# A weight stream's buffers moved to 224 bytes beyond a multiple of 256

## The chip, the cores and the metric

The kernel runs on one core of one Trainium2 chip. The metric is device time in microseconds from the first to the last instruction of one execution with what lies around them, the median over several executions. Smaller is better. Before the change it is 773.04 us (three runs, 772.54 to 774.1).

## The reference, cut to what matters

One hybrid encoder layer over 512 tokens and 16 meta tokens, width 1024, all in float32:

```python
h = rmsnorm(x, mix_norm)
na_q, na_k, na_v, df_q, df_k, df_v, g_na, g_df = split(h @ w_in)      # 40 blocks of 128 columns
o_na = neighbourhood_attention(na_q, na_k, na_v, na_rpb) @ w_na_out   # 8 heads of 64
o_df = diff_attention(rope(df_q), rope(df_k), df_v, lam) @ w_diff_out # 4 heads, two softmaxes each
x = x + (sigmoid(g_na) * o_na + sigmoid(g_df) * o_df) @ w_o
h = rmsnorm(x, ffn_norm)
x = x + (silu(h @ w_gate) * (h @ w_up)) @ w_down                      # D_FF = 2816
return rmsnorm(x, final_norm)[:, 16:]
```

## The kernel before

Every activation is kept transposed, with 128 channels on the partitions and the tokens along the row. Every large product is written as three matmuls in a rounded float32 type: operands are split into a rounded half (`whi`, `xh`, `mh` and so on) and a remainder (`wlo`, `xl`, `ml`), and `mm3` issues high by high (L140), high by low (L142) and low by high (L144) into one accumulator. In a matmul the weight block is loaded into the array (a LDWEIGHTS on PEld), and the activation is streamed through it (the MATMUL on PE): in `pg<-xh,wlo` the output is `pg`, the stream `xh`, the loaded weights `wlo`.

The work has these stages:

- Attention. Eight units (four heads of differential attention, four pairs of neighbourhood attention) in turn; beside each runs the dense projection of the next: k and v (`pk`, `pv`, tokens in two runs of 256 and 272 columns), q (`pq`, 512) and a gate block (`pg`, 512). A generator hands out dense steps between attention slots.
- `diff_out` (`pd`), the other branch's projection (`pn`) and the output projection (`po`), all with 512 columns.
- SwiGLU: for each of 22 blocks of 128 columns, seven half-size products (256 columns) from the operands `xb` (Strassen's scheme over gate and up weights).
- Down projection (`pdn`, 512 columns; the last block in two halves, `pdh`, 256 columns), then the final norm.

The pool `wp` is the weight stream. A piece of 128 x 1024 floats (512 KB) is loaded by SyncE into one of three buffers of the tag `wraw` (as `wraw`, as `fG` for the gate weights of the SwiGLU, as `draw` for the down weights). ACT then writes its rounded half and DVE the remainder:

```python
raw = self.wp.tile([P, 8, P], F32, name="wraw", tag="wraw", bufs=3)
hi = self.wp.tile([P, 8, P], F32R, name="whi", tag="whi", bufs=2)
lo = self.wp.tile([P, 8, P], F32R, name="wlo", tag="wlo", bufs=2)
nc.scalar.copy(hi[:, k:k + h], raw[:, k:k + h])
eng.tensor_tensor(out=lo[:, k:k + h], in0=raw[:, k:k + h], in1=hi[:, k:k + h].bitcast(F32), op=ALU.subtract)
```

In attention and the projections all loaded weights are `whi` and `wlo`. In the SwiGLU two of the seven products (`PB11` into `pa`, `PB21` into `pb`) use them; the other five use tiles of a pool `F` (`fwh`, `fsh`, `fdh` and their remainders). In the down projection the first two pieces lie in them (as `dhi`, `dlo`), the others in a ring (`wring`).

Where tiles lie. Pools are stacked from the low end of each partition: constants, small tiles, `wp` at byte 10,496 = 41 x 256, then the pools after it. Other pools are stacked from the high end, under a pad of 56 floats that brings them to multiples of 256. All buffers of `wp` are of 4096 bytes, so each begins on a multiple of 256. So do the streamed operands: rows of `xh` and `xl` are padded to 576 floats (2304 bytes), `mh`, `ml`, `onh`, `odh`, `gh` and `gl` are of whole multiples. The exception is `xb`, which starts 8 floats into its tile; the ring takes the same space from its start:

```python
xbt = [XB.tile([P, nxb + 64], F32R, name="xb", tag=t) for t in ("xbh", "xbl")]
xbh, xbl = (t[:, 8:8 + nxb].rearrange("p (i k n) -> p i k n", i=7, k=4) for t in xbt)
```

Of the kernel before, what the change touches and what calls it, by code (L numbers as in the profile page):

```python
# [10 lines left out]
F32 = mybir.dt.float32  # L11
# [7 lines left out]
P = 128  # L19
# [52 lines left out]
class Kernel:  # L72
# [665 lines left out]
    def run(self):  # L738
        tc, nc, a = self.tc, self.nc, self.a
        es = ExitStack()  # L740
        self.cp = es.enter_context(tc.tile_pool(name="cp", bufs=1))
        self.sm = es.enter_context(tc.tile_pool(name="sm", bufs=1))
        self.wp = es.enter_context(tc.tile_pool(name="wp", bufs=1))
        sA2 = ExitStack()
        A2 = sA2.enter_context(tc.tile_pool(name="A2", bufs=1))
        self.od = A2.tile([P, 4, T], F32, name="od")
        self.onh = A2.tile([P, 4, T], F32R, name="onh")
        self.onl = A2.tile([P, 4, T], F32R, name="onl")
        self.gates = A2.tile([P, 8, T], F32, name="gates")
        sA1 = ExitStack()  # L750
        self.A1 = sA1.enter_context(tc.tile_pool(name="A1", bufs=1))
        sat = ExitStack()
        self.attn = sat.enter_context(tc.tile_pool(name="attn", bufs=1))

        rp = es.enter_context(tc.tile_pool(name="rp", bufs=1, side="right"))
        nc.gpsimd.memset(rp.tile([P, 56], F32, name="pad"), 0.0)
        self.sstg = ExitStack()
        self.stg = self.sstg.enter_context(tc.tile_pool(name="stg", bufs=1, side="right"))
        self.sM2 = ExitStack()
        sps = ExitStack()  # L760
        self.pjp = sps.enter_context(tc.tile_pool(name="pjp", bufs=3, space=PSUM))
        self.tp = sps.enter_context(tc.tile_pool(name="tp", bufs=2, space=PSUM))
        self.mp = sps.enter_context(tc.tile_pool(name="mp", bufs=1, space=PSUM))
        self.sp = sps.enter_context(tc.tile_pool(name="sp", bufs=1, space=PSUM))

        self.setup()
        self.sts = [dict() for _ in range(8)]
        self.late = False
        self.cur = -1

        self.bms = []
        for _ in self.dense_first():
            pass
        self.stream = self.stream_a()
        for i in range(8):
            st = self.sts[i]
            self.drain_until(lambda: "ready" in st)
            self.cur = i
            for s in range(8):
                for fn in self.pend.pop(self.slot, []):  # L780
                    fn()
                self.fill(FILL_A)
                if i % 2 == 0:
                    self.d_scores(i // 2, st, s)
                    if s in (1, 4):
                        self.bms.append(self.build_bm(i + (s == 4)))
                else:
                    self.n_scores(i // 2, st, s)
                self.fill(FILL_B)
                self.slot += 1  # L790
        while self.pend:
            for fn in self.pend.pop(self.slot, []):
                fn()
            self.fill(FILL_A + FILL_B)
            self.slot += 1
        self.late = True
        for _ in self.stream:
            pass
        sat.close()
        sps.close()  # L800
        sA1.close()
        self.phase_b(sA2)
        self.sM2.close()
        es.close()
# [414 lines left out]
```

## Time and profile before

| | |
|---|---|
| median of 3 runs | 773.04 us (772.54 to 774.1) |
| profiled execution, its time | 773.11 us |
| its span, first to last instruction | 771.3 us |
| mean granted TensorE clock | 0.986 |
| attention with its projections | up to 320 us |
| `pd`, `pn`, `po` | 320 to 408 us |
| SwiGLU | 408 to 632 us |
| down projection and final norm | 634 to 771 us |

The span is what the trace covers; the 1.8 us that the execution takes beyond it lie around the first and last instruction. In the rows of the profile that follow, times are in microseconds from the start of the span, and means of one instruction are in nanoseconds. A matmul's duration is a latency: the next one starts before it ends, so how fast a row of matmuls goes is read from their starts.

### The profile page before, as it was taken

To read this page: it belongs to the slowest core of one execution; us is meant where nothing else is said; L and a number is where in the kernel's file an instruction comes from. 1 tells how busy PE (TensorE), PEld (TensorE's weight loads), DVE (VectorE), ACT (ScalarE), POOL (GpSimd) and SP (SyncE) were. 2 spreads that over 40 slices of the span, in tenths; PEclk is the share of its full clock that TensorE was granted. 3 is DMA by queue.
4 is the path that set the end of the run, shared out by engine and by line. 5 is a ranking of instruction groups with operands and counts; after the bars stand their busy time and mean duration, and the time that the engine had idled before them with its cause. 6 is when DMAs were issued, how large, how long until landed. Compare 5 with 4: busy or idle time off the path is not lost.

```text
span 771.3 us, 12598 instructions
## 1 busy us (share of the span) xinstructions
PE 748.6 (97%) x4794; PEld 674.1 (87%) x4794; DVE 575.6 (75%) x1053; ACT 379.7 (49%) x669; POOL 55.3 (7%) x141
## 2 busy tenths in 40 slices
PE   7999999999999999999998999999999989999995
PEld 5899889998889888878887999999999987888884
DVE  5777897788788867648889899999999959632214
ACT  6345545545554546514554655555555556422201
POOL 2030110110011000001121000000000000000100
PEclk8999999999999999999998999999999999999998
DMA  7474643453563412235541333333333232633003
GB/s 261 136 182 143 158 123 103 123 152 104 137 159 101 121 58 80 82 110 163 169 132 42 110 110 110 110 107 104 104 104 108 66 102 68 206 103 95 1 1 109
DMA packets 34715, 87.88 MB, mean 114 GB/s; under 512 B 4512, under 2 KB 6576, under 8 KB 34656
## 3 DMA queue, kind: packets, MB, share of 16 engines
q1 hardware_dynamic: 32688, 82.97, 35.6%
q0 software_dynamic: 1136, 3.34, 1.5%
q8 instruction: 37, 0.61, 0.3%
q10 hardware_dynamic: 832, 0.79, 0.3%
q14 instruction: 22, 0.18, 0.1%
HBM read 70.01 MB, written 2.10 MB: 93 GB/s over the span
## 4 chain that ended last, share of the span: by engine, by line
PE 85%; DVE 9%; DMA 2%; issue 1%; ACT 1%; SPq 0%; DVEq 0%; ACTq 0%
PE pdn L144 4%; PE pdn L140 4%; PE pdn L142 4%; PE pa L140 4%; PE pa L144 4%; PE pb L140 4%; PE pg L140 4%; PE pa L142 4%; PE pb L142 4%; PE pb L144 4%; PE pg L144 4%; PE pg L142 4%; PE s L513 2%; PE pv L140 2%; PE pv L142 2%; PE pv L144 2%
## 5 line engine op out<-in xcount | busy, mean ns | idle before, releaser
L117 ACT CAST whi<-wraw 128x1024 fp32r<-128x1024 f32 (+1 forms) x57 | 58.9, 1033 | 56.9 <-PE pd L142 13.1
L118 DVE TENSOR_TENSOR wlo<-wraw,whi 128x1024 fp32r<-128x1024 f32 (+1 forms) x57 | 68.5, 1201 | 17.2 <-ACT whi L117 16.9
L144 PE MATMUL pdn<-gh,wring 128*128 128x512 f32 x138 | 53.8, 390 | 1.3 <-DVE wring L155 1.3
L140 PE MATMUL pdn<-gh,wring 128*128 128x512 f32 x138 | 53.8, 390 | 0.0
L142 PE MATMUL pdn<-gl,wring 128*128 128x512 f32 x138 | 53.7, 389 | 0.0
L140 PE MATMUL pg<-xh,whi 128*128 128x512 f32 x128 | 52.6, 411 | 0.4 <-DVE vt L379 0.4
L142 PE MATMUL pg<-xl,whi 128*128 128x512 f32 x128 | 50.6, 395 | 0.0
L144 PE MATMUL pg<-xh,wlo 128*128 128x512 f32 x128 | 50.2, 393 | 0.0
L155 DVE TENSOR_TENSOR wring<-draw,wring 128x1024 fp32r<-128x1024 f32 (+1 forms) x22 | 24.7, 1126 | 28.8 <-ACT wring L154 28.8
L154 ACT CAST wring<-draw 128x1024 fp32r<-128x1024 f32 (+1 forms) x22 | 21.0, 974 | 45.9 <-PE pdn L142 34.5
L154 ACT CAST fdh<-fG 128x1024 fp32r<-128x1024 f32 x22 | 23.2, 1056 | 36.8 <-PE pa L142 34.7
L154 ACT CAST ath<-tp 128x256 fp32r<-128x256 f32 (+1 forms) x48 | 20.5, 443 | 42.2 <-PE tp L637 22.0
L1137 POOL TENSOR_TENSOR ssq<-ssq,sq 128x512 f32<-128x512 f32 x11 | 16.4, 1493 | 345.6 <-ACT sq L1136 335.2
L155 DVE TENSOR_TENSOR wlo<-fG,whi 128x1024 fp32r<-128x1024 f32 x22 | 26.9, 1224 | 14.4 <-ACT whi L154 14.4
L517 ACT ACTIVATE e<-s,m 128x528 f32<-128x528 f32 x32 | 22.5, 704 | 23.0 <-DVE m L515 22.7
L144 PEld LDWEIGHTS pdn<-gh,wring 128*128 128x128 f32 x138 | 25.9, 188 | 7.1 <-DVE wring L155 1.7
L140 PE MATMUL pk<-xh,whi 128*128 128x256 f32 (+1 forms) x128 | 28.9, 303 | 3.1 <-ACT xh L244 3.1
L140 PEld LDWEIGHTS pdn<-gh,wring 128*128 128x128 f32 x138 | 25.9, 188 | 5.6 <-ACT wring L154 0.2
L142 PEld LDWEIGHTS pdn<-gl,wring 128*128 128x128 f32 x138 | 25.9, 188 | 5.3
L155 DVE TENSOR_TENSOR fwl<-fW,fwh 128x1024 fp32r<-128x1024 f32 x22 | 26.9, 1225 | 3.1 <-ACT fwh L154 3.1
L144 PEld LDWEIGHTS pg<-xh,wlo 128*128 128x128 f32 x128 | 24.0, 188 | 5.2
L621 ACT ACTIVATE en<-en,m 128x272 f32<-128x272 f32 x32 | 16.7, 522 | 24.1 <-DVE m L619 23.8
(292 smaller groups left out, 2596.2 us busy)
## 6 DMA issues: line engine op xcount, KB each, us to landing
wraw<-in_w_in_dram SPq DMA_DIRECT2D x39, 512.0 KB, 3.8
fG<-in_w_gate_dram SPq DMA_DIRECT2D x22, 512.0 KB, 3.5
kd<-khl SPq DMA_DIRECT2D x32, 264.0 KB, 4.2
draw<-in_w_down_dram SPq DMA_DIRECT2D x16, 512.0 KB, 3.6
fW<-in_w_up_dram SPq DMA_DIRECT2D x22, 256.0 KB, 2.6
fV<-in_w_up_dram SPq DMA_DIRECT2D x22, 256.0 KB, 2.9
qs<-qhl SPq DMA_DIRECT2D x32, 128.0 KB, 2.8
wraw<-in_w_o_dram SPq DMA_DIRECT2D x8, 512.0 KB, 3.5
```

The costliest lines, as they stand in the source:

```text
L117: nc.scalar.copy(hi[:, k:k + h], raw[:, k:k + h])
L118: eng.tensor_tensor(out=lo[:, k:k + h], in0=raw[:, k:k + h], in1=hi[:, k:k + h].bitcast(F32), op=ALU.subtract)
L140: nc.tensor.matmul(outs[i], wh, rhs[i][0], start=start, stop=False, **kw)
L142: nc.tensor.matmul(outs[i], wh, rhs[i][1], start=False, stop=False, **kw)
L144: nc.tensor.matmul(outs[i], wl, rhs[i][0], start=False, stop=stop, **kw)
L154: self.nc.scalar.copy(hi, src)
L155: self.nc.vector.tensor_sub(lo, src, hi.bitcast(F32))
L513: nc.tensor.matmul(sc[:, r0:r1], qs[:, q], kd[:, p, r0:r1], start=p == 0, stop=p == 1)
L517: nc.scalar.activation(e, sc, AF.Exp, bias=m, accum_out=l[:, c:c + 1])
L621: x = nc.scalar.activation(e[:, :n], e[:, :n], AF.Exp, bias=m, scale=-1.0, accum_out=l[:, 0:1])
L1137: (nc.gpsimd if m < n - 1 else nc.vector).tensor_tensor(out=ssq, in0=ssq, in1=sq, op=ALU.add)
```

## The change

A pad of 56 floats (224 bytes) becomes the first tile of `wp`, and a pool with a pad of 8 floats (32 bytes) follows `wp`. The stream's seven buffers then begin at 10,720 and every 4096 bytes after it, 224 bytes beyond a multiple of 256; what is stacked behind them begins 256 bytes higher than before, on the same place within 256. Tiles at the high end stay. The pads are written once each by POOL, as the allocator wants a tile that is used.

```diff
         self.cp = es.enter_context(tc.tile_pool(name="cp", bufs=1))
         self.sm = es.enter_context(tc.tile_pool(name="sm", bufs=1))
         self.wp = es.enter_context(tc.tile_pool(name="wp", bufs=1))
+
+        nc.gpsimd.memset(self.wp.tile([P, 56], F32, name="wpad"), 0.0)
+        wpe = es.enter_context(tc.tile_pool(name="wpe", bufs=1))
+        nc.gpsimd.memset(wpe.tile([P, 8], F32, name="wpad2"), 0.0)
         sA2 = ExitStack()
         A2 = sA2.enter_context(tc.tile_pool(name="A2", bufs=1))
```

On PE, DVE, ACT and SyncE the instructions and their order are those of before. POOL's order before, from the kernel's first instructions to the setup of the constants (`vec` holds the norm weights):

```order
L1203 MEMSET const-uint8-127 128x1
L1212 UNCONDITIONAL_BRANCH
L756 MEMSET pad 128x56
L214 DMA vec<-in_vec_dram 128x25
L262 MEMSET ones_d 128x1
```

And now, at the same place:

```order
L1207 MEMSET const-uint8-127 128x1
L1216 UNCONDITIONAL_BRANCH
L745 MEMSET wpad 128x56
L747 MEMSET wpad_69 128x8
L760 MEMSET pad 128x56
L214 DMA vec<-in_vec_dram 128x25
L262 MEMSET ones_d 128x1
```

The two new MEMSETs stand ahead of the load of `vec`; lines behind the change are numbered four higher.

## The prediction

> **What bounds the kernel now.** I read the page first: the busy shares, then the chain of work that ended last.
>
> ```profile
> PE 748.6 (97%) x4794; PEld 674.1 (87%) x4794; DVE 575.6 (75%) x1053; ACT 379.7 (49%) x669; POOL 55.3 (7%) x141
> ...
> PE 85%; DVE 9%; DMA 2%; issue 1%; ACT 1%; SPq 0%; DVEq 0%; ACTq 0%
> ```
>
> TensorE is busy 97% of the span and is 85% of the chain. Busy matmuls overlap, so I next took the table by stage. Its columns are the stretch, its length, then busy time and instruction count of PE, PEld, DVE, ACT and POOL, then the granted clock, the DMA share and GB/s.
>
> ```profile
> 33.00:320.00 287.00, 286.69 (x1797) 254.15 (x1798) 231.43 (x584) 152.18 (x321) 29.45 (x92) 1.00 0.44 123
> 364.70:408.00 43.30, 43.30 (x193) 35.85 (x192) 36.47 (x49) 25.56 (x40) 8.21 (x7) 1.00 0.44 141
> 423.00:630.00 207.00, 207.00 (x1771) 206.52 (x1770) 182.85 (x226) 118.07 (x192) 0.00 (x0) 1.00 0.32 104
> 650.00:742.00 92.00, 92.00 (x408) 76.14 (x407) 33.88 (x38) 26.39 (x31) 6.95 (x5) 1.00 0.33 99
> ```
>
> These are attention with its projections, the output projection, the SwiGLU products and the down projection. PE is full in all four at clock 1.00, so the kernel's time is the number of matmuls times the time from one start to the next. That step is what a moved operand could change, and I read it from start times in the timeline (first and last of a run; the count between them follows each row pair).
>
> ```profile
> 700.21 0.39 PE L140 MATMUL pdn<-gh,wring 128*128 128x512 f32 x1
> ...
> 702.93 0.39 PE L140 MATMUL pdn<-gh,wring 128*128 128x512 f32 x1
> ```
> ```profile
> 307.41 0.39 PE L142 MATMUL pg<-xl,whi 128*128 128x512 f32 x1
> ...
> 308.57 0.39 PE L140 MATMUL pg<-xh,whi 128*128 128x512 f32 x1
> ...
> 310.83 0.39 PE L142 MATMUL pg<-xl,whi 128*128 128x512 f32 x1
> ```
> ```profile
> 747.22 0.28 PE L140 MATMUL pdh<-gh,wring 128*128 128x256 f32 x1
> ...
> 748.06 0.28 PE L142 MATMUL pdh<-gl,wring 128*128 128x256 f32 x1
> ```
> ```profile
> 500.03 0.28 PE L140 MATMUL pa<-xb,fsh 128*128 128x256 f32 x1
> ...
> 501.43 0.28 PE L140 MATMUL pb<-xb,whi 128*128 128x256 f32 x1
> ```
> ```profile
> 120.05 0.41 PE L140 MATMUL pv<-xh,whi 128*128 128x256 f32 x2
> ...
> 122.49 0.28 PE L142 MATMUL pv<-xl,whi 128*128 128x256 f32 x1
> ```
>
> - 512 columns, steady: 12 steps in 2.72 us, 226.7 ns each.
> - 512 columns just after other work: 5 steps in 1.16 us, 232 ns; the next 10 take 2.26 us, 226 ns. After a break the row needs some five matmuls to settle.
> - 256 columns in the last block (`pdh`): 7 steps in 0.84 us, 120.0 ns.
> - 256 columns in the SwiGLU (`xb`): 12 steps in 1.40 us, 116.7 ns.
> - 256 and 272 columns alternating (`pk`, `pv`): 10 pairs in 2.44 us, 244 ns a pair.
>
> From 226.7 and 120.0 a column costs 106.7/256 = 0.417 ns, and a matmul 13.3 ns besides. The same sum leaves 10.0 ns for `xb`, 18.6 ns for the unsettled 512s, and 12.0 ns for each of a pair. The kernel tells `xb` from `pdh` by one thing that bears on this change: `xb` starts 8 floats (32 bytes) into a tile that lies on a multiple of 256, while `gh` and `gl` lie on one. So where the streamed (moving) operand lies seems to be worth 3.3 ns a matmul. The change moves the other operand, the loaded weights.
>
> **The change part by part.** *Which matmuls read a moved tile.* The `whi`/`wlo` (and `dhi`/`dlo`) halves feed them. The rows below are one of three products each (L140, L142, L144), columns as on the page.
>
> ```profile
> L144 PE MATMUL pg<-xh,wlo 128*128 128x512 f32 x128 | 50.2, 393 | 0.0
> L144 PE MATMUL pa<-xb,wlo 128*128 128x256 f32 x88 | 25.1, 285 | 0.0
> L144 PE MATMUL pq<-xh,wlo 128*128 128x512 f32 x64 | 25.1, 392 | 0.0
> L144 PE MATMUL po<-mh,wlo 128*128 128x512 f32 x64 | 24.9, 389 | 0.0
> L144 PE MATMUL pb<-xb,wlo 128*128 128x256 f32 x88 | 24.6, 279 | 0.0
> L144 PE MATMUL pk<-xh,wlo 128*128 128x256 f32 x64 | 18.5, 289 | 0.0
> L144 PE MATMUL pv<-xh,wlo 128*128 128x256 f32 x64 | 18.2, 284 | 0.0
> L144 PE MATMUL pn<-onh,wlo 128*128 128x512 f32 x32 | 12.5, 389 | 0.0
> L144 PE MATMUL pd<-odh,wlo 128*128 128x512 f32 x32 | 12.4, 389 | 0.0
> L144 PE MATMUL pdn<-gh,dlo 128*128 128x512 f32 x16 | 6.2, 390 | 0.0
> ```
>
> With 512 columns: (128+64+64+32+32+16) x 3 = 1008. In pairs: `pk` and `pv`, 64 of 256 columns and as many of 272, x 3: 768. In the SwiGLU: (88+88) x 3 = 528, two of its seven products. That is 2304 of 4794; the rest, the ring weights of the down projection above all, stay where they were.
>
> *The weight load itself.* One row has loads at odd places already: the mean square of x reads 88-column slices of one tile, so that slice c begins 352c bytes in, at 0, 96, 192, 32, 128 and 224 bytes beyond a multiple of 256.
>
> ```profile
> 25.56 0.70 PEld L181 LDWEIGHTS ms<-ones_d,ssq 128*88 128x88 f32 x8 [0.18 <-issue]
> ```
> ```profile
> L181 PEld LDWEIGHTS ms<-ones_d,ssq x20: 153/158/333, 25.6 to 417.9; 128*88 128x88 f32 x12, 128*128 128x128 f32 x8
> ```
>
> Eight loads (two for each slice) in 0.70 us: less the last one's 0.158, 7 steps of 77 ns. The 12 loads have a median of 158 and a minimum of 153 (the row's maximum is of its 128-column form). None stands out, so a load that begins 32 or 224 bytes off costs nothing that shows when it runs alone. Beside 512 columns a load has room: PEld is busy 76.14 of the 92.00 us of the down projection. Beside 256 it has none to spare, at 206.52 of 207.00 us in the SwiGLU. What is not shown is a wide stream and a shifted load together. Bounds, in ns a matmul: as the settled and unsettled 512s differ, +5.3 on 1008, +5.3 us; as `pdh` and `xb` differ in the good direction, -3.3 on 1008 and 12.0 to 10.0 on 768, -3.4 - 1.5 = -4.9 us. I take 0, the row of loads alone being nearest to what is moved: the weights.
>
> *The splits that write the halves.* ACT casts 80 pieces (56 of attention and the projections, 22 of the gate weights, 2 of the down weights) and DVE subtracts as many, now from and to shifted tiles. `xb` is written at 32 bytes off, `mh` and `wring` are not:
>
> ```profile
> L154 ACT CAST mh<-m 128x512 fp32r<-128x512 f32 x8 | 5.0, 621 | 15.0 <-DVE m L838 15.0
> L154 ACT CAST xb<-xg 128x512 fp32r<-128x512 f32 x4 | 2.4, 604 | 0.0
> L155 DVE TENSOR_TENSOR xb<-xt,xb 128x768 fp32r<-128x768 f32 x4 | 3.8, 955 | 1.8 <-ACT xb L154 1.8
> L155 DVE TENSOR_TENSOR wring<-draw,wring 128x768 fp32r<-128x768 f32 x8 | 7.7, 958 | 10.8 <-ACT wring L154 10.8
> ```
>
> 604 against 621 and 955 against 958: nothing on either engine, and both lie beside PE.
>
> *The transfers.* All of `wraw`, `fG` and `draw` now land off a multiple of 256.
>
> ```profile
> wraw<-in_w_in_dram SPq DMA_DIRECT2D x39, 512.0 KB, 3.8
> ```
> ```profile
> SPq L104 <- DVE wlo L118: 142.1, 32, 8.3
> ```
> ```profile
> ACT whi L117 <- DMA wraw<-in_w_in_dram: 4.9, 2, 3.5
> ```
> ```profile
> 2.13 6.98 DMA wraw<-in_w_in_dram
> ```
>
> A piece lands 3.8 us after its issue, but the queue waited 142.1 us for DVE to free a buffer, so the stream runs ahead of its use; ACT waited for it twice, 4.9 us. In the output projection a piece is used each 43.3/8 = 5.4 us with three buffers. Even at twice 3.8 us it would be there in time. The queue is in order, so what stands behind a slower piece (the copies of k and q) would start later by the same, with the same slack. The one landing on the path is the first piece, 6.98 us of the start. Bounds: 0, and, for a tenth more on 6.98, 0.7 us. I take 0: nothing in the rows shows a landing that depends on its place. The Trainium skill, DMA: Bandwidth & Descriptors, "How a descriptor splits into AXI transactions", speaks against the change: a transfer that starts off a 256-byte boundary pays for a whole first transaction. By that, an estimate: 4096 bytes from 224 on make 17 transactions of 135 beats in place of 16 of 128, 5.5% more; on the first landing 0.4 us, so that the sum would be 773.5. The waits above show why it would end there; no row of this profile shows packets by their place.
>
> *Two MEMSETs on POOL,* ahead of the load of `vec`:
>
> ```profile
> 0.74 0.14 POOL L756 MEMSET pad<- 128x56 f32 x1 [0.29 <-POOLq L1203]
> 1.30 0.68 POOL L214 DMA_DIRECT2D vec<-in_vec_dram  x1 [0.41 <-issue]
> ```
> ```profile
> vec<-in_vec_dram POOLq DMA_DIRECT2D x1, 12.5 KB, 3.6
> ```
>
> At most 0.14 us each, less where they overlap as POOL's others do. `vec` is wanted by ACT's first scaling, which stands behind the cast of the piece that lands at 2.13 + 6.98 = 9.1 us; issued at 1.30 and landed 3.6 us later, it has some 4 us to spare. Nothing. *The tiles behind the stream* move by 256 bytes, the same place within 256, and the settled step is the same for operands at many multiples of it: nothing.
>
> **Sum.** 773.11 us for the profiled execution (span 771.3 and 1.8 around it) + 0 = 773.1; the median of the runs, 773.04, is 0.07 below it, which I neglect.
>
> **The rivals.**
> 1. *Slower: the shifted load keeps the 512-column rows from settling.* The five steps of 232 ns show that such a state exists with nothing else different; if the load's place decides it, the state would last. For it: 512-column matmuls are the ones that settle to a better step. Against it: the load has long ended before the next matmul starts. 1008 x 5.3 = +5.3: 778.4. It decides when the step of `po` stays over 228.
> 2. *Slower: the load of the SwiGLU's two products takes longer beside a stream.* PEld has no slack there; 116.7 would become 120.0 as for `pdh`: 528 x 3.3 = +1.7, 774.8.
> 3. *Faster: it is the distance between stream and weights that counts.* `xb` lies 32 bytes ahead of its weights modulo 256; with the weights at 224, `xh`, `mh` and the others lie just so too. Then each matmul's 13.3 (pairs 12.0) would become 10.0: -4.9, 768.2; if only the pairs gain, -1.5, 771.6. Against it: nothing separates the distance from the place of the stream alone, and the loads alone show no effect. The Trainium skill, TensorE: Matmul & The Clock Gate, "Step-by-step: what each phase is for", says that weights and stream have independent read ports and that a load does not steal from the running matmul. By that rule neither 1 nor 3 could come and the time would be the forecast's; no row here shows it either way.
>
> **How the numbers follow.** What a measurement of this kernel can tell from no change is about 0.2%, 1.5 us. Forecast (773.1, with the landing term up to 773.8): 0.45, the most, since the loads alone are the only rows with the moved operand off its place. Rival 1: 0.21; rival 2: 0.11, its 1.7 being just past the bound; rival 3: 0.23, of which a third gains only on the pairs and ends near the bound. So faster 0.22, same 0.46, slower 0.32. The range reaches to both outer cases, 768.2 and 778.4, as each is likelier than one in ten; what is left out is a sum of a rival and a transfer term beyond them: 768.0 to 778.6. The forecast alone: 772.5 to 774.1, its terms and the spread of the runs shown (772.54 to 774.1).
>
> **What the profile after would show.** Steps: 226.7 in `po`, 120.0 in `pdh`, 116.7 in `pb` from `wlo`, 244 a pair in `pv`, all as now; 228 or more in `po` is rival 1, 120 in the `wlo` products of the SwiGLU alone is rival 2, 223 or 240 a pair is rival 3. The casts of ACT and the subtractions of DVE keep their means. A landing time of `wraw` over 3.8 us with more than 4.9 us of ACT's waits would show the transfers at work. I would be wrong if the weights' place within 256 sets the step of a matmul in either direction.

## The result, and the profile after

| | before | after |
|---|---|---|
| median | 773.04 us (7 runs, 772.39 to 774.1) | 776.43 us (7 runs, 775.32 to 778.65) |
| ratio to before | | 1.0048, interval 1.0033 to 1.0063 |
| profiled execution, span | 771.3 us | 774.5 us |

The kernel became slower by 3.4 us. The busy shares and the chain of the changed kernel's page:

```profile
PE 753.2 (97%) x4794; PEld 674.3 (87%) x4794; DVE 575.7 (74%) x1053; ACT 379.4 (49%) x669; POOL 55.8 (7%) x143
...
PE 90%; DVE 7%; ACT 1%; DMA 1%; issue 1%; SPq 0%; DVEq 0%; ACTq 0%
```

PE has 4.6 us more busy time with the same 4794 matmuls (748.6 before), and the chain runs through it more than before; DVE, ACT and PEld are where they were. So each matmul takes longer, and the table by stage shows it at once when stretches of equal length are compared. First before, then after: `diff_out` (`pd`), output projection (`po`), SwiGLU. What matters is the count of matmuls, the second number of the PE column.

```profile
321.00:341.00 20.00, 20.00 (x90) 16.57 (x89) 9.74 (x11) 3.74 (x5) 0.00 (x0) 1.00 0.31 98
367.00:407.00 40.00, 40.00 (x178) 33.11 (x177) 33.30 (x45) 23.02 (x36) 7.67 (x6) 1.00 0.45 145
440.00:620.00 180.00, 180.00 (x1545) 180.00 (x1545) 163.44 (x203) 103.54 (x169) 0.00 (x0) 1.00 0.33 106
```
```profile
321.00:341.00 20.00, 20.00 (x88) 16.05 (x87) 9.86 (x12) 3.95 (x5) 0.00 (x0) 1.00 0.28 84
367.00:407.00 40.00, 40.00 (x173) 32.10 (x173) 32.90 (x45) 22.05 (x36) 8.39 (x7) 1.00 0.46 148
440.00:620.00 180.00, 180.00 (x1531) 180.00 (x1530) 164.07 (x204) 102.39 (x166) 0.00 (x0) 1.00 0.32 103
```

The granted clock is 1.00 in all six, and in the same 40 us 173 matmuls of `po` fit in place of 178, in the same 180 us 1531 of the SwiGLU in place of 1545. The steps, from start times in the timeline as in the prediction: first `po` before, then `po` and other rows of the changed kernel.

```profile
390.01 0.39 PE L142 MATMUL po<-ml,whi 128*128 128x512 f32 x1
...
392.73 0.39 PE L142 MATMUL po<-ml,whi 128*128 128x512 f32 x1
```
```profile
390.17 0.39 PE L142 MATMUL po<-ml,whi 128*128 128x512 f32 x1
...
392.97 0.39 PE L142 MATMUL po<-ml,whi 128*128 128x512 f32 x1
```
```profile
307.38 0.39 PE L142 MATMUL pg<-xl,whi 128*128 128x512 f32 x1
...
308.55 0.39 PE L140 MATMUL pg<-xh,whi 128*128 128x512 f32 x1
...
310.88 0.39 PE L142 MATMUL pg<-xl,whi 128*128 128x512 f32 x1
```
```profile
120.00 0.40 PE L144 MATMUL pv<-xh,wlo 128*128 128x256 f32 x2
...
122.16 0.41 PE L144 MATMUL pv<-xh,wlo 128*128 128x256 f32 x2
```
```profile
700.27 0.39 PE L144 MATMUL pdn<-gh,wring 128*128 128x512 f32 x1
...
702.99 0.39 PE L144 MATMUL pdn<-gh,wring 128*128 128x512 f32 x1
```

- `po`: 12 steps in 2.80 us, 233.3 ns (before, 12 in 2.72 us, 226.7). The single steps repeat 231, 235, 233, 234 to the end of the row.
- `pg`: the first 5 steps 234 ns, the next 10 again 233 ns. Before, the row settled to 226 after five; now it never does.
- `pv`: 9 pairs in 2.16 us, 240 ns a pair (244 before): faster.
- `pdn` from the ring, whose weights and stream did not move: 12 steps in 2.72 us, 226.7 ns, as before.
- SwiGLU: 117.8 ns in the mean of each of the seven products (116.7 before), also in the five whose weights did not move.

The loads themselves are not longer by their records. Before, then after (count, then us busy, mean ns of one):

```profile
L144 PEld LDWEIGHTS po<-mh,wlo 128*128 128x128 f32 x64 | 12.0, 188 | 2.5
```
```profile
L144 PEld LDWEIGHTS po<-mh,wlo 128*128 128x128 f32 x64 | 12.0, 187 | 2.9
```

Transfers and splits give nothing. Of the changed kernel, the landing of `wraw` and ACT's casts from it (count, then us busy, mean ns); 3.8 us of landing as before, and ACT's wait for a piece is 4.5 us, 4.9 before:

```profile
wraw<-in_w_in_dram SPq DMA_DIRECT2D x39, 512.0 KB, 3.8
```
```profile
L117 ACT CAST whi<-wraw 128x1024 fp32r<-128x1024 f32 x55 | 57.6, 1048 | 55.0 <-PE pd L142 13.6 <-PE pk L142 10.7 <-PE pg L142 7.7
L117 ACT CAST whi<-wraw 128x512 fp32r<-128x512 f32 x2 | 1.2, 618 | 4.5 <-DMA wraw<-in_w_in_dram 4.5
```

Where the time went, from the first start of each stage in the two timelines:

| stage | before | after | difference |
|---|---|---|---|
| to the first `pd` | 319.98 | 320.22 | +0.24 |
| first `pd` to the first SwiGLU product | 88.16 | 90.71 | +2.55 |
| to the broadcast matmul `rp` early in the SwiGLU | 28.03 | 27.07 | -0.96 |
| `rp` to the last SwiGLU product | 196.74 | 198.57 | +1.83 |
| to the last matmul | 131.98 | 131.73 | -0.25 |

The second line is 384 matmuls (`pd`, `pn`, `po`) x 6.6 ns = 2.5. The first is a sum of two signs: 576 matmuls of `pg` and `pq`, 230 ns in the mean before and 233 after, make +1.7, and 768 of the pairs at some -1.5 make -1.2. The third holds the waits at the start of the SwiGLU and a stretch in which the clock was granted at 0.50 and matmuls step at 213 ns in both kernels; it took 26.7 to 30.0 us in the eleven traces of this case, so its -0.96 need not be an effect of the change. The fourth is 1,680 matmuls x 1.1 ns. In the fifth the 48 matmuls of `pdn` that read `dhi` and `dlo` do step slower in the changed kernel (some 233 ns for 227), and the clock was granted at 0.50 for 3.4 us there, as it was not before. Neither shows in the time: before, PE then stood idle for 1.3 us until DVE had written a remainder of the ring, and now it has no such wait.

### The profile page after: what moved, and what is told of

It is laid out like the page before. It is cut to its first block, busy times and chain, and to the rows that moved or that the text cites. A ratio compares the mean times of both kernels' runs of the same rounds, so it can differ in the third digit from the quotient of the medians.

```text
span 774.5 us, 12600 instructions
## 1 busy us (share of the span) xinstructions
PE 753.2 (97%) x4794; PEld 674.3 (87%) x4794; DVE 575.7 (74%) x1053; ACT 379.4 (49%) x669; POOL 55.8 (7%) x143
## 4 chain that ended last, share of the span: by engine, by line
PE 90%; DVE 7%; ACT 1%; DMA 1%; issue 1%; SPq 0%; DVEq 0%; ACTq 0%
PE pdn L142 5%; PE pdn L144 5%; PE pdn L140 4%; PE pa L140 4%; PE pa L144 4%; PE pa L142 4%; PE pg L140 4%; PE pb L142 4%; PE pb L140 4%; PE pb L144 4%; PE pg L142 4%; PE pg L144 4%; PE s L513 2%; PE pv L140 2%; PE pv L142 2%; PE pv L144 2%
```

## Experiments

Two theories stood against each other after the result. **Place:** a load, a stream or a transfer that begins off a multiple of 256 is slower in itself. **Distance:** the step of a matmul depends on where its weights begin minus where its stream begins, modulo 256 (in what follows "the distance"; before, it is 0 in all 512-column products and the pairs, and 224 in the SwiGLU, where `xb` begins at 32). The times of before beside the runs were 772.61 us for the first four and 773.16 and 772.86 us for the others.

**1. The raw buffers alone.** `wraw`, `fG` and `draw` at 224, `whi` and `wlo` pushed back to multiples of 256 by a pad between them.

```diff
+        nc.gpsimd.memset(self.wp.tile([P, 56], F32, name="wpad"), 0.0)     # ahead of wraw
+        nc.gpsimd.memset(self.wp.tile([P, 8], F32, name="wmid"), 0.0)      # ahead of whi
```

> Only the landing buffers (wraw, fG, draw) lie 224 bytes beyond a multiple of 256; the halves whi and wlo lie on multiples. If the loss comes from the weight loads beside the stream, nothing is left of it: ratio 1.000 +- 0.0015, step of po 226.7 ns, pairs of pv 244 ns. If it comes from the transfers, or from reading the landing buffers on ACT and DVE, the whole of it is here: ratio 1.004 to 1.005, with po still at 226.7.

Measured: 772.35 us, ratio 0.9996 (0.9983 to 1.0008). `po`, in the same stretch as above:

```profile
367.00:407.00 40.00, 40.00 (x178) 33.14 (x177) 33.24 (x45) 23.21 (x36) 7.70 (x6) 1.00 0.45 145
```

178 again. Transfers into shifted tiles and reads of them by ACT and DVE cost nothing here.

**2. The halves alone.** `whi` and `wlo` at 224, the raw buffers on multiples of 256.

```diff
+        nc.gpsimd.memset(self.wp.tile([P, 56], F32, name="wmid"), 0.0)     # ahead of whi
+        wpe = es.enter_context(tc.tile_pool(name="wpe", bufs=1))
+        nc.gpsimd.memset(wpe.tile([P, 8], F32, name="wpad2"), 0.0)
```

> The other half: whi and wlo at 224, landing buffers on multiples of 256. Weight loads beside the stream: the whole loss, ratio 1.0048, po 233, pairs 240. Transfers: ratio 1.000.

Measured: 778.01 us, ratio 1.0061 (1.0046 to 1.0076); `po` and the SwiGLU as in the changed kernel:

```profile
367.00:407.00 40.00, 40.00 (x173) 32.14 (x172) 32.96 (x45) 21.97 (x36) 8.40 (x7) 1.00 0.46 150
440.00:620.00 180.00, 180.00 (x1531) 180.00 (x1530) 164.12 (x204) 102.56 (x166) 0.00 (x0) 1.00 0.32 103
```

The whole loss is in the halves, that is, in what TensorE loads. The ratio's interval overlaps that of the changed kernel, 1.0033 to 1.0063.

**3. The changed kernel with its streams moved as well.** `xh`, `xl`, `onh`, `onl`, `mh` and `ml` also at 224: for `po`, `pn`, `pg`, `pq` and the pairs the distance is 0 again, with weights and stream both off a multiple of 256. The streams of `pd` and the SwiGLU's `xb` stay.

```diff
-        self.xh = A1.tile([P, KT, LP], F32R, name="xh")[:, :, :LT]
+        self.xh = A1.tile([P, KT * LP + 64], F32R, name="xh")[:, 56:56 + KT * LP].rearrange("p (k n) -> p k n", k=KT)[:, :, :LT]
...
```

> The changed kernel, and the streamed operands xh, xl, onh, onl, mh, ml also begin 224 bytes beyond a multiple of 256 (odh, odl stay). If the distance between weights and stream counts: po, pn, pq, pg settle at 226.7 again, pd stays at 233, pairs go back to 244, and the time is within 0.1% of before but for the SwiGLU. If the place of the weights alone counts: po stays at 233. If each operand off its place costs by itself: po above 233 and the ratio above 1.005.

Measured: 774.77 us, ratio 1.0028 (1.0016 to 1.0039). `pd`, `po`, SwiGLU:

```profile
321.00:341.00 20.00, 20.00 (x87) 16.05 (x87) 9.51 (x11) 3.41 (x4) 0.00 (x0) 1.00 0.29 97
367.00:407.00 40.00, 40.00 (x177) 32.91 (x176) 31.76 (x43) 21.72 (x34) 8.01 (x7) 1.00 0.45 145
440.00:620.00 180.00, 180.00 (x1530) 180.00 (x1530) 164.02 (x204) 102.66 (x166) 0.00 (x0) 1.00 0.32 103
```

`po` is back at 177 (227.0 ns in the mean), `pn` at 227.1, `pg` at 229.9, the pairs at 121.9 in the mean, as before; `pd`, whose stream stayed, keeps 233.4, and the SwiGLU 117.8. The loss goes where the distance goes back to 0 and stays where it does not: `pd`'s 96 x 6.6 ns = 0.6 us and the SwiGLU's 1.8 make 2.4, beside the 2.2 measured.

**4. A scan.** Streams as before; each piece of weights begins at a place of its own.

```diff
+    def whalf(self, name, tag, byte):
+        t = self.wp.tile([P, 8 * P + 32], F32R, name=name, tag=tag, bufs=2)
+        o = (byte - 128 * (self.nw[tag] % 2)) % 256 // 4
+        self.nw[tag] += 1
+        return t[:, o:o + 8 * P].rearrange("p (k n) -> p k n", k=8)
...
-        hi = self.wp.tile([P, 8, P], F32R, name="whi", tag="whi", bufs=2)
-        lo = self.wp.tile([P, 8, P], F32R, name="wlo", tag="wlo", bufs=2)
+        hi, lo = (self.whalf(n, n, self.wbyte[i]) for n in ("whi", "wlo"))
...
-        g = hilo(G, [P, 2, 4, P], ("whi", "wlo"), 2, self.wp)
+        g = [self.whalf(n, n, self.gbyte[f]).rearrange("p (i k) n -> p i k n", i=2) for n in ("whi", "wlo")]
```

> The halves of each piece begin at a place of their own within 256 bytes: in po the eight pieces at 0, 224, 32, 160, 96, 192, 64, 128, the same set over the pieces of pd and pn, and over the gate pieces of the SwiGLU, beside streams that stay. If only places off a multiple of 64 disturb: po 226.7 at 0, 64, 128 and 192, about 233 at 32, 96, 160 and 224. If any place off a multiple of 256 does: 226.7 at 0 alone. In the SwiGLU, where xb lies at 32: if the distance counts, the products with weights at 32 go towards the 120.0 ns of pdh; if the place of the stream alone does, they stay at 116.7.

One execution, 776.40 us. Mean steps in ns by distance (of `po` the 23 steps within a piece; of a SwiGLU product 12 steps, the last one to the next product):

| distance | 0 | 32 | 64 | 96 | 128 | 160 | 192 | 224 |
|---|---|---|---|---|---|---|---|---|
| `po` | 226.7 | 233.1 | 233.3 | 234.3 | 232.2 | 233.4 | 228.9 | 233.3 |
| pairs (`pk`, `pv`) | 122.0 | 122.5 to 123.0 | 120.2 | 120.6 | 123.0 | | | |
| SwiGLU, gate weights | 119.6 | 118.6 | 117.9, 113.7 | 117.6 | 118.7 | 119.6 | 117.9, 113.7 | 116.7 |

512 columns settle only at distance 0; 192 is the nearest. At 256 columns other distances are better. At distance 0 the SwiGLU's gate products go from 116.7 to 119.6, towards the 120.0 of `pdh`, so it was the distance and not the place of `xb` alone that made them quicker. That places count modulo 256 is in these numbers too: 128 is not as good as 0, and from one block to the next of `pg` the weights advance by 512 bytes and the stream by 2304, so that the difference passes through odd multiples of 256, and before the change the row settles at 226 ns all the same. All places tried are multiples of 32 bytes.

At two distances the SwiGLU shows two values (the 117.9 at 192 is of a block ahead of `rp`, in which the unmoved products step so too). The gate weights at distance 192, as in the changed kernel, made this row of the scan (start times of a `pb`, and of the unmoved products shortly ahead of it):

```profile
529.73 0.28 PE L152 MATMUL pb<-xb,fwh 128*128 128x256 f32 x1
...
531.13 0.28 PE L152 MATMUL pc<-xb,fwh 128*128 128x256 f32 x1
...
533.92 0.28 PE L152 MATMUL pb<-xb,whi 128*128 128x256 f32 x1
...
535.17 0.28 PE L156 MATMUL pb<-xb,wlo 128*128 128x256 f32 x1
```

12 steps of unmoved products in 1.40 us, 116.7 ns; 11 steps of the moved one in 1.25, 114 ns (113.3 by the finer times of the trace; the table's 113.7 has the step to the next product in it). In the changed kernel the same distance gives 117.8, and the unmoved products step at 117.8 too. Step by step the two are repeating patterns: 116, 118, 120, 113 is the one of before, 119, 119, 116, 118 the other. Before also has the second one, from 423 us to the `rp` at 436.17, and the first one after it; the changed kernel comes out of its own `rp` with unmoved products at 116.7, and from a moved one at 444.5 us on all are in the second, to the end of the stage. To the end of the stage it is so in all three profiled executions in which the gate weights alone lie at 192 (the changed kernel, experiments 2 and 3), and in none of the four with every product at 224 (before, experiments 1, 5 and 8). So what a distance sets seems to be which patterns can last, and which of them holds to be carried over from what went before.

**5. The streams alone.** Weights where they were, the six streams of experiment 3 moved on by 32 bytes: distance 224, as in the changed kernel, with no load shifted.

```diff
-        self.xh = A1.tile([P, KT, LP], F32R, name="xh")[:, :, :LT]
+        self.xh = A1.tile([P, KT * LP + 64], F32R, name="xh")[:, 8:8 + KT * LP].rearrange("p (k n) -> p k n", k=KT)[:, :, :LT]
...
```

> The kernel before with its weights where they were and the streams xh, xl, onh, onl, mh and ml moved on by 32 bytes, so that weights minus stream is 224 modulo 256, as in the changed kernel, with nothing shifted in the weights. Theory, the distance alone counts: po and pn step at 233.3 ns, pg and pq at 233, the pairs' pv at 120.3 (mean of both kinds), pd (its streams odh and odl stay) at 226.7, SwiGLU at 116.7. Sum: (64 + 32) x 3 x 6.6 = +1.9, 576 x 3 = +1.7, 768 x -1.6 = -1.2: +2.4, 775.0 us. Rival, the place of the weights itself slows the matmul: all steps as before, 772.6.

Measured: 774.84 us, ratio 1.0018 (1.0006 to 1.003).

```profile
321.00:341.00 20.00, 20.00 (x90) 16.55 (x89) 10.25 (x12) 4.37 (x5) 0.00 (x0) 1.00 0.28 85
367.00:407.00 40.00, 40.00 (x174) 32.10 (x173) 32.97 (x45) 22.09 (x35) 8.41 (x7) 1.00 0.45 148
440.00:620.00 180.00, 180.00 (x1545) 180.00 (x1545) 164.55 (x204) 103.59 (x168) 0.00 (x0) 1.00 0.32 106
```

`po` and `pn` step at 233.3, `pg` and `pq` at 233.1, the pairs at 120.6; `pd` and the SwiGLU are as before, all as the distance says. The time rose by 1.7 us where 2.4 were expected. Place is out for the load, as weights at 224 step slowly in the changed kernel and well in 3, and weights at 0 well before and slowly here; and for the stream, as a stream at 0 steps well before and slowly in the changed kernel.

**6 and 7. `xb` alone.** One number: `xb` begins at 64, or at 192, in place of 32, which gives all seven products distance 192, or 64.

```diff
-            xbh, xbl = (t[:, 8:8 + nxb].rearrange("p (i k n) -> p i k n", i=7, k=4) for t in xbt)
+            xbh, xbl = (t[:, 16:16 + nxb].rearrange("p (i k n) -> p i k n", i=7, k=4) for t in xbt)     # 48 in run 7
```

> The kernel before with one number changed: xb begins 64 bytes into its tile and not 32, so that in all seven SwiGLU products weights minus stream is 192 modulo 256 in place of 224. This is the distance that the gate weights' two products have in the changed kernel (117.8 ns there, 113.7 ns in two blocks of the scan). Theory, the step is a repeating pattern that the distance allows, and the one it falls into depends on what went before: either 113.7 on 1848 matmuls, -5.5 us, 767.1, or 117.8, +2.0, 774.6, and the same step in nearly all of the stage. Rival, what costs in the changed kernel's SwiGLU is the place of the weights and not the distance: 116.7 and 772.6.

> As the run before it, with xb 192 bytes into its tile: weights minus stream is 64 modulo 256, at which the scan showed 117.9 and 113.7 ns. Theory: 113.7, 767.1, or 117.9, 774.8. Rival: 116.7, 772.6.

Measured: 775.26 us, ratio 1.0019 (1.0003 to 1.0035), and 768.53 us of three runs (766.06, 768.53, 773.32), ratio 0.9954 (0.9908 to 1.0). The SwiGLU of the one and of the other:

```profile
440.00:620.00 180.00, 180.00 (x1530) 180.00 (x1530) 164.02 (x203) 102.78 (x167) 0.00 (x0) 1.00 0.32 104
```
```profile
440.00:620.00 180.00, 180.00 (x1589) 179.94 (x1589) 167.38 (x208) 103.63 (x172) 0.00 (x0) 1.00 0.33 106
```

Distance 192 fell into 117.8 ns, as the changed kernel's did; distance 64, in the profiled execution, into 113.3, 59 more matmuls in 180 us. That its three runs lie 7 us apart, with 1,680 matmuls x 4.5 ns = 7.6 us between the two patterns, suggests that it does not fall into the same one each time; the other two runs left no step times.

**8. The pairs alone.** The halves of the `k` and `v` pieces 64 bytes on, all others on multiples of 256.

```diff
+        hi, lo = (self.whalf(n, n, 64 if i < 32 and i % 2 == 0 else 0) for n in ("whi", "wlo"))
```

> The kernel before with the halves of the k and v pieces alone 64 bytes on; those of all other pieces stay on multiples of 256. Theory: the pairs of 256 and 272 columns step at 120.3 on the mean in place of 121.9, 768 x -1.6 = -1.2 us, 771.4, and all 512-column steps stay. Rival, the scan's faster pairs came from what ran beside them: 121.9 and 772.6.

Measured: 771.61 us, ratio 0.9977 (0.9965 to 0.9989): faster than both kernels. The pairs in the timeline, 8 in 1.92 us, 240 ns a pair:

```profile
120.73 0.40 PE L150 MATMUL pv<-xh,wlo 128*128 128x256 f32 x2
...
122.65 0.40 PE L148 MATMUL pv<-xl,whi 128*128 128x256 f32 x2
```

**9. Three distances.** Runs 7 and 8 together, and the three ring pieces of the last block 64 bytes on, so that `pdh` has distance 64 too.

```diff
+            self.ring = [[r[:, o:o + 7 * 8 * P].rearrange("p (i k n) -> p i k n", i=7, k=8) for r in ring]
+                         for o in (0, 16)]
...
-                hi, lo = (r[:, (j - 2) % 7] for r in self.ring)
+                hi, lo = (r[:, (j - 2) % 7] for r in self.ring[m == KT - 1])
```

> The kernel before with three distances set by what the runs so far showed, and nothing else: xb 192 bytes into its tile (as e7: 113.3 ns in 1848 products of the SwiGLU), the halves of the k and v pieces at 64 (as e8: 120.2 on the mean in 768 matmuls), and the three ring pieces of the last block at 64, so that pdh reads weights 64 bytes beyond its stream (132 matmuls, 120.0 before). All 512-column products keep distance 0. Theory: 1848 x -3.4 = -6.3, 768 x -1.7 = -1.3, 132 x -6.7 = -0.9: -8.5 from some 773, 764.5 us; where a run's SwiGLU falls into a slower pattern, as the spread of e7 (766.1 to 773.3) makes likely for some, up to 771. Rival, the gains are made up elsewhere (clock, waits): over 771 in all runs with the steps as named.

Measured: median 771.93 us of 12 runs, ratio 0.9963 (0.9936 to 0.999). Four runs lie at 763.9 to 767.0, eight at 771.4 to 774.8, none between; the 17 of before lie at 771.3 to 775.3. So the 764.5 that was expected came in four of twelve, and the median gained 0.9 us. The profiled execution, 773.7 us, is one of the eight, with the SwiGLU at 117.8; the four left no step times. In its last block both patterns stand within 10 us, under one and the same distance (`msa`, `ms` and `rp` are other matmuls between):

```profile
748.75 0.28 PE L148 MATMUL pdh<-gl,wring 128*128 128x256 f32 x1
...
753.46 0.28 PE L150 MATMUL pdh<-gh,wring 128*128 128x256 f32 x1
753.93 0.28 PE L187 MATMUL ms<-ones_d,sq 128*128 128x1 f32 x2
...
755.22 0.28 PE L148 MATMUL pdh<-gl,wring 128*128 128x256 f32 x1
...
757.60 0.28 PE L148 MATMUL pdh<-gl,wring 128*128 128x256 f32 x1
757.71 0.59 PE L974 MATMUL rp<-dg,ones 128*128 128x256 f32 x2
...
758.38 0.28 PE L148 MATMUL pdh<-gl,wring 128*128 128x256 f32 x1
...
760.50 0.28 PE L148 MATMUL pdh<-gl,wring 128*128 128x256 f32 x1
```

40 steps in 4.71 us, 117.8 ns; after the two short breaks by `ms` 21 steps in 2.38 us, 113.3; after the break by `rp` 18 steps in 2.12 us, 117.8 again. The pattern changed across breaks of a few hundred nanoseconds, twice in this trace. What decides which one comes out of a break stays open.

## Why the prediction was right in its range and wrong in its mechanism

The time, 776.43 us, lies in the stated range, 768.0 to 778.6. That is no merit of the forecast: the range was drawn to reach the outer rivals on both sides, while the forecast itself, 773.1 with no step changed, and its own narrower range, 772.5 to 774.1, did not come. The sign named for being wrong came, as moving the weights within 256 changed the step, and in both directions. That the time stayed inside is partly luck: the losses alone come to some 6.0 us (4.2 in the 512s and 1.8 in the SwiGLU, below), 779.0 and beyond the range, and a gain of the pairs that the forecast had not either took some of it back.

**The step that failed** is the one for what was "not shown", a wide stream and a shifted load together: "I take 0, the row of loads alone being nearest to what is moved: the weights". The row of `ms` loads showed a load that runs beside no wide stream; the effect is one of weights and stream together, so that row could not speak to it. The prediction's own bounds were nearer, and of each a part came: +5.3 ns on the 512s (measured +6.6 in `pd`, `pn` and `po`, +3 in `pg` and `pq`), and -2.0 on the pairs (measured some -1.5). The argument against rival 1, that a load has long ended before the next matmul starts, looked at the wrong matmul. Before the change a load of `po` runs from 390.01 us for 0.19, beside the stream that started at 390.01, and the matmul that uses it starts at 390.24: it ends only just ahead of the one, and lies beside the other.

- *Rival 1* had the mechanism of the 512s: they no longer settle, and `po` at 233.3 is over its point of 228. Its term was 1008 x 5.3 = 5.3 us; measured 2.55 + 1.7 = 4.2, with nothing from the 48 matmuls of `pdn`. But what keeps the rows from settling is not the load's place, as it supposed: with weights at 224 and streams at 224 they settle (experiment 3). The step of the steady stages was sized too low, while a part of attention's rows had not settled before either (230 ns in the mean).
- *Rival 3* had the cause, the distance, and its case of the pairs alone came: -1.2 for -1.5. That each product would gain was wrong: what is good for 256 columns (224 better than 0) is bad for 512 (233.3 against 226.7). The prediction carried a figure from `xb` with 256 columns over to 512.
- *Rival 2* placed the SwiGLU's cost on the two moved products at 3.3 ns, 1.7 us. It came as +1.1 ns on all seven, +1.8 us: the right size with another mechanism, a pattern that lasts over products whose operands did not move.
- Rivals 1, 2 and 3 were given chances as if only one could come. They are one mechanism in three places, and all came at once: +4.2 - 1.2 + 1.8 = 4.8, less 1.2 in the stretches at the start of the SwiGLU and behind it, 3.6 beside the 3.4 measured. As the first of these stretches differs from run to run, that the two agree so well is partly chance.

**The terms that held.** Transfers, casts, subtractions and MEMSETs at 0 (experiment 1: 0.9996); the ring's `pdn` at 226.7; PE as the bound of each stage. For transfers the Trainium skill, DMA: Bandwidth & Descriptors, "How a descriptor splits into AXI transactions", has a transfer that does not start on a multiple of 256 bytes fetch and pay for a whole first transaction; by the prediction's estimate, 5.5%. The page speaks of bytes that are fetched, and what moved here is where they land. `wraw` lands in 3.8 us in both kernels and in 3.7 with the raw buffers alone moved, so it doesn't show here.

**The rule that spoke for the forecast.** The Trainium skill, TensorE: Matmul & The Clock Gate, "Step-by-step: what each phase is for", has a load that takes no read bandwidth from the running matmul, by independent ports. Read as the prediction read it, that no place of the weights changes the step, the runs disagree: with as many loads, streams and the same clock, 226.7 against 233.3 ns by the distance alone (experiments 3 and 5). Why the distance counts, no run here shows; nor whether it counts to the stream of the load's own matmul or to the one that runs beside the load, as within a product both lie alike.

## What to carry to other kernels

Where TensorE is full, read its step from start times and ask for each shape how far weights and stream begin from each other modulo 256: move one of the two by some floats and read the step again. Keep 512-column products at distance 0, and look for another distance where products are 256 wide (64 for the pairs: 0.9977 of this kernel's time). These distances were read for this rounded float32 type with weights of 128 x 128; for others they are to be read anew. A row that shows one operand alone is no evidence for the two together, and rivals that are one mechanism at several widths are to be summed.

## What the hardware showed that was not expected

- The step of a stream of matmuls is a short repeating pattern (231, 235, 233, 234 ns at 512 columns and distance 224, 231, 231, 238 at 160; 116, 118, 120, 113 or 119, 119, 116, 118 at 256 columns), and the same code can hold different ones: 113.3 or 117.8 ns at distance 64.
- A pattern can outlive what brought it: in the changed kernel five products with unmoved weights step at 117.8 in place of 116.7 beside two that moved. It need not: in the scan the unmoved ones go back to 116.7 right behind a moved one at 113.3.
- The run times of experiment 9 fall into two groups, 763.9 to 767.0 and 771.4 to 774.8 us, at the same granted clock (0.983 to 0.986). The two patterns of the SwiGLU would make a gap of that size: run 7 took 766.1 us with 113.3 ns, run 9 773.7 us with 117.8. That each of the twelve executions fell by its pattern is not shown.
